# Turning the mixed values of three groups by DMA transposes in two 16-bit planes instead of on TensorE

## The chip, the cores and the metric

The kernel runs on one core of one Trainium2 chip. The metric is device time in microseconds, as the median of several executions; beside it stands one execution taken by the hardware profiler, whose rows are quoted here. The engines are TensorE (PE, with its weight loads PEld), VectorE (DVE), ScalarE (ACT), GpSimd (POOL) and SyncE (SP). SP computes nothing; it issues nearly all DMAs, in order. Each engine runs its own list of instructions in order and waits on semaphores of the others.

## What is computed

One layer of a decoder on 256 tokens of width 2048, float32. Cut to the part around the change:

```python
h = rmsnorm(x, norm_mix_w)
q, k, v, z, b_raw, a_raw, p_in, g_a, g_b = split(h @ w_in)
# q, k, v: causal convolution of width 4, silu; q, k normalised
o   = gated_delta_rule(q, k, v, g_log, beta)            # 16 heads of 128
y_a = rmsnorm(o, gdn_norm_w) * silu(z)
y_b = (trailing means of p_in, 4 groups of 512) @ pool_w[group] * pool_scale
mixed = sigmoid(g_a) * y_a + sigmoid(g_b) * y_b         # 256 x 2048
x = x + mixed @ w_out
# then: rmsnorm, gated MLP of 5632 with a causal convolution, w_down, final rmsnorm
```

## The kernel before

**Products of two parts.** TensorE multiplies in a rounded format (`F32R`). To keep float32 accuracy every operand is held as a high part (the value rounded) and a low part (the rest), and a product is the sum of high x high, low x high and high x low. Activations are split once. Weights are split as they stream: SP loads a weight tile of 256 rows by 512 columns (512 KB) into `raw` (line 122, four buffers), ACT makes `whi` by a cast (line 141, three buffers), DVE makes `wlo` as the difference (line 149, three buffers). This happens in `begin`, called by `weights`, two tiles ahead of use (`AHEAD`, line 29). A raw buffer comes free when its `wlo` is made; a `whi` or `wlo` buffer when PE has used the tile.

**GEMMs.** `gemm_a` (lines 168 to 186) goes through the weight tiles of a product with 512 output columns: for each tile twelve matmuls, lines 179 to 181, of which only line 181 reads `wlo`. The first matmul of a tile therefore waits for ACT's cast, the third for DVE's difference. A GEMM over the width of 2048 has eight tiles.

**Order of the groups.** The mixer runs in four groups `g` of four heads (512 channels). A group runs GEMMs for k, q, v, pooling input, gate b, the pooling weights, z and gate a. Work that hangs on a GEMM's result is not placed right behind it but put on a list, `later`, whose entries are called inside the next GEMM, when its second weight tile begins. A second list, `side_work`, holds the delta rule of the group (`gdn`) as a generator, of which a step is taken with every half tile. A scheduler then orders each engine's instructions by its own estimates of their times; the call order above is what it starts from, and tiles of a pool are given out in that order.

**The place of the change.** When a group's delta rule is done, `gated` (line 901) forms the group's mixed values in `sz` with two DVE operations (lines 903 and 904): 128 partitions, two token tiles `t`, 512 channels. The output projection needs them with channels on the partitions. `mixed` (line 913), put on `later` for groups 0 to 2 (line 920) and called at once for group 3, does that: `turned` (line 216) makes eight TensorE transposes of 128x128 into two PSUM tiles from the pool `psg` (line 224; four buffers, used by the delta rule and the convolutions too), ACT casts each PSUM tile to the high part `mhi` (line 916) and DVE subtracts for the low part `mlo` (line 917). Both are read first by the two unfinished output GEMMs `early`, after all four groups' GEMMs. `turned` is also used by `conv_silu` for the results `ev` of the k and q GEMMs.

**Queues.** SP's list holds, in order, the raw loads; per group two loads of convolution weights (`taps`, line 573) into the buffers named `sz` and `yb`; a store of v to memory and three shifted loads back (lines 855 and 587); and small copies of the delta rule through memory (`cdd`, `lb`, `tbd`, `TT`: lines 703, 706, 725, 728). Buffers of the pool `mp` have one copy for most names: `ga0` holds decayed products of the group's delta rule, `yb` the pooled branch, both free once `sz` is formed and taken again by the next group's taps or delta rule.

Of the kernel before, what the change touches and what calls it, by code (L numbers as in the profile page):

```python
# [6 lines left out]

F32 = mybir.dt.float32
F32R = mybir.dt.float32r
I32 = mybir.dt.int32  # L10
AF = mybir.ActivationFunctionType
ALU = mybir.AluOpType

P = 128
S = 256
# [18 lines left out]
def kernel(  # L34
# [20 lines left out]
    nc = tc.nc  # L55
# [11 lines left out]
    def nm(s):  # L67
        cnt[0] += 1
        return f"{s}_{cnt[0]}"

    def pg(shape=(P, 512)):
        return psg.tile(list(shape), F32, tag="g", name=nm("psg"))
# [85 lines left out]
    def drain():  # L158
        for _ in side_work[0]:
            pass  # L160
# [5 lines left out]
    later = []  # L166

    def gemm_a(lh, ll, nk, steps=None, ps=None):

        ps = pm() if ps is None else ps  # L170
        for c in range(nk // 2) if steps is None else steps:
            if c == 1:
                while later:
                    later.pop(0)()
            hi, lo = weights()
            for kk in range(2):
                k = 2 * c + kk
                for t in range(2):
                    mm(ps[:, t, :], lh(k, t), hi[:, kk, :], start=(k == 0), stop=False)  # L179
                    mm(ps[:, t, :], ll(k, t), hi[:, kk, :], start=False, stop=False)  # L180
                    mm(ps[:, t, :], lh(k, t), lo[:, kk, :], start=False, stop=(k == nk - 1))  # L181
                side()
        return ps
# [32 lines left out]
    def turned(src):  # L216

        out = []
        for f2 in range(2):
            pt = pg([P, 2, S])  # L220
            for ff in range(2):
                f = 2 * f2 + ff
                for t in range(2):
                    nc.tensor.transpose(pt[:, ff, t * P : (t + 1) * P], src[:, t, f * P : (f + 1) * P], ident)
            out.append(pt)
        return out


# [20 lines left out]
    mp = mix.__enter__()  # L249
# [193 lines left out]
    for g, w in enumerate(WINDOWS):  # L443
# [13 lines left out]
                            op=ALU.add)  # L457
# [100 lines left out]
    def evict(ps, by=None):  # L558

        by = rs1 if by is None else by  # L560
        e = mp.tile([P, 2, 512], F32, tag="ev", bufs=1, name=nm("ev"))
        for t in range(2):
            nc.scalar.activation(e[:, t, :], ps[:, t, :], AF.Copy, scale=by[:, t : t + 1])
        return e
# [25 lines left out]
    def v_conv(g, vt):  # L590

        vt = vt.rearrange("p t h d -> p t (h d)")
        for j, m in zip((2, 1, 0), moved_of[g]):
            nc.vector.tensor_tensor(m, m, taps_of[g][j], op=ALU.mult)
            nc.vector.tensor_tensor(vt, vt, m, op=ALU.add)
            yield
        th = mp.tile([P, 2, 512], F32, tag="th", name=nm("th"))
        nc.scalar.activation(th, vt, AF.Tanh)
        yield
        nc.vector.scalar_tensor_tensor(vt, th, 1.0, vt, op0=ALU.add, op1=ALU.mult)  # L600
        yield

    def conv_silu(e, kind, g, dst):

        pts = turned(e)
        y = mp.tile([P, 4, S], F32, tag="cy", bufs=2, name=nm("cy"))
        for f in range(4):
            r = kind * 16 + 4 * g + f
            gs = pts[f // 2][:, f % 2, :]

            def w(j):
                return cqw[:, j * 48 + r : j * 48 + r + 1]

            nc.scalar.activation(y[:, f, :], gs, AF.Copy, scale=w(3))
            for j in (2, 1, 0):
                s = 3 - j
                nc.vector.scalar_tensor_tensor(y[:, f, s:], gs[:, : S - s], w(j), y[:, f, s:],
                                               op0=ALU.mult, op1=ALU.add)
        th = mp.tile([P, 4, S], F32, tag="th", name=nm("th"))
        nc.scalar.activation(th, y, AF.Tanh)  # L620
        k_conv.append(nc.vector.scalar_tensor_tensor(dst, th, 1.0, y, op0=ALU.add, op1=ALU.mult).ins)
# [214 lines left out]
    for g in range(4):  # L836
        kq = mp.tile([P, 4, 2, S], F32, tag="kq", bufs=1, name=nm("kq"))
        for kind, dst in ((1, kq[:, :, 0, :]), (0, kq[:, :, 1, :])):
            ps = ps_k0 if kind == 1 and g == 0 else gemm_a(xh, xl, KD)
            e = evict(ps)  # L840
            later.append(lambda e=e, kind=kind, g=g, dst=dst: conv_silu(e, kind, g, dst))

        vt = mp.tile([P, 2, 4, P], F32, tag="vt", name=nm("vt"))
        vt2 = vt.rearrange("p t h d -> p t (h d)")
        res = []
        later.append(lambda g=g, kq=kq, vt=vt, res=res: side_work.__setitem__(0, gdn(g, kq, vt, v_conv(g, vt), res)))
        v_taps(g)
        if g == 0:
            def after_k(k_conv=k_conv[0]):
                with tc.issue_after(last_pow[0]), tc.issue_after(k_conv):  # L850
                    fixed_parts()

            later.append(after_k)
        e = evict(gemm_a(xh, xl, KD), rsh)
        nc.sync.dma_start(vrow[g, SH : SH + S, :].rearrange("(t p) d -> p t d", p=P), e)
        later.append(lambda e=e, g=g, vt2=vt2: v_moved(e, g, vt2))


        win = WINDOWS[g]
        psb = scales(g)  # L860
        ps = gemm_a(xh, xl, KD)
        e = evict(ps)
        phi = mtile(g, [P, 4, S], F32R, nm("phi"))
        plo = mtile(4 + g, [P, 4, S], F32R, nm("plo"))

        def pooled(e=e, g=g, phi=phi, plo=plo):
            for f2 in range(2):
                pt = pg([P, 2, S])
                for ff in range(2):
                    fs = slice((2 * f2 + ff) * P, (2 * f2 + ff + 1) * P)  # L870
                    mm(pt[:, ff, P:S], e[:, 1, fs], bands[:, g, P + PAD : NB], start=True, stop=False,
                       skip_group_check=True)
                    mm(pt[:, ff, 0 : P + PAD], e[:, 0, fs], bands[:, g, 0 : P + PAD], start=False, stop=True,
                       skip_group_check=True)
                fs = slice(2 * f2, 2 * f2 + 2)
                nc.scalar.copy(phi[:, fs, :], pt)
                nc.vector.tensor_tensor(plo[:, fs, :], pt, phi[:, fs, :].bitcast(F32), op=ALU.subtract)

        later.append(pooled)

        def gate(ps, tag):
            th = mp.tile([P, 2, 512], F32, tag=tag, name=nm("gate"))
            for t in range(2):
                nc.scalar.activation(th[:, t, :], ps[:, t, :], AF.Tanh, scale=rsh[:, t : t + 1])
            return th

        tb = gate(gemm_a(xh, xl, KD), "th")
        ps = gemm_a(lambda k, t: phi[:, k, t * P : (t + 1) * P], lambda k, t: plo[:, k, t * P : (t + 1) * P], 4)
        yb = mp.tile([P, 2, 512], F32, tag="yb", name=nm("yb"))
        nc.vector.tensor_tensor(yb, ps, psb.unsqueeze(1).to_broadcast([P, 2, 512]), op=ALU.mult)  # L890
        nc.vector.scalar_tensor_tensor(yb, tb, 1.0, yb, op0=ALU.add, op1=ALU.mult)

        ps = gemm_a(xh, xl, KD)
        sz = mp.tile([P, 2, 512], F32, tag="sz", name=nm("sz"))
        nc.vector.scalar_tensor_tensor(sz, gate(ps, "th"), 1.0, ps, op0=ALU.add, op1=ALU.mult)
        ta = gate(gemm_a(xh, xl, KD), "th")
        nc.vector.scalar_tensor_tensor(sz, ta, 1.0, sz, op0=ALU.add, op1=ALU.mult)
        sz4 = sz.rearrange("p t (h d) -> p (t h) d", h=4)
        nc.vector.tensor_tensor(sz4, sz4, gwb.unsqueeze(1).to_broadcast([P, 8, P]), op=ALU.mult)

        def gated(sz=sz, res=res, yb=yb):
            drain()
            nc.vector.tensor_tensor(sz, res[0].rearrange("p t h d -> p t (h d)"), sz, op=ALU.mult)
            nc.vector.tensor_tensor(sz, sz, yb, op=ALU.add)

        if g < 3:
            gated()
        mh = mtile(g, [P, 4, S], F32R, f"mhi{g}")
        ml = mtile(4 + g, [P, 4, S], F32R, f"mlo{g}")
        mhi.append(mh)  # L910
        mlo.append(ml)

        def mixed(sz=sz, mh=mh, ml=ml):
            for f2, pt in enumerate(turned(sz)):
                fs = slice(2 * f2, 2 * f2 + 2)
                nc.scalar.copy(mh[:, fs, :], pt)
                nc.vector.tensor_tensor(ml[:, fs, :], pt, mh[:, fs, :].bitcast(F32), op=ALU.subtract)

        if g < 3:
            later.append(mixed)  # L920

    def at(tiles):
        return lambda k, t: tiles[k // 4][:, k % 4, t * P : (t + 1) * P]
# [46 lines left out]
    for c in range(DFF // 512):  # L970
# [4 lines left out]
        for f in range(4):  # L975
# [3 lines left out]
            for j in (1, 0):  # L979
                s = 2 - j  # L980
# [114 lines left out]
```

## Time and profile before

| | |
|---|---|
| median of 3 executions | 1572.16 us (1571.49 to 1575.03) |
| the profiled execution, own time | 1572.57 us |
| its span, first to last instruction | 1570.8 us |
| granted TensorE clock, mean | 0.998 |
| share of the 16 DMA engines' time by SP's queue | 61.0% |
| data moved | 304.23 MB, 194 GB/s |

The page gives busy times per engine, and the span in 40 slices of 39 us with the busy share of each in tenths. A timeline row is: start in us from the span's start, length, engine, line, operation, output and inputs, shapes, count. A row of a group by line is: line, engine, operation, tile names, shapes, count, then busy us and mean ns of one, then the idle time ahead of it and what ended that. Lengths of PE rows are those of pipelined matmuls, which overlap; the distance between two starts is what one costs. The three turns of mixed values on PE begin at 243.8, 420.8 and 599.1 us; that of group 3 at 769 to 771 us.

### The profile page before, as it was taken

The page shows a single profiled execution, that of the slowest core. Times are in us where ns is not written, and L with a number is a line of the kernel's source. Part 1 is how long each engine was busy: PE and PEld are TensorE (multiplying, and loading weights), DVE is VectorE, ACT ScalarE, POOL GpSimd, SP SyncE. Part 2 cuts the span into 40 slices and gives each one's busy share as a digit, 9 for nine tenths or more (in the row PEclk, how much of TensorE's full clock was granted, in tenths as well). Part 3 has the DMA queues.
Part 4 walks back from the last instruction along what each step waited for, and adds up shares of the span by engine and source line. Part 5 has one row for each costly group of instructions (what it writes and reads, how often), then busy time and mean ns, then how long its engine had stood idle before and what let it go on. Part 6 is the DMA issues. An engine that isn't in the chain of part 4 may idle for free.

```text
span 1570.8 us, 21247 instructions
## 1 busy us (share of the span) xinstructions
PE 1558.3 (99%) x8022; PEld 1308.1 (83%) x8022; DVE 1077.4 (69%) x1647; ACT 744.7 (47%) x956; POOL 47.4 (3%) x69
## 2 busy tenths in 40 slices
PE   9999999999999999999999999999999999999997
PEld 8878888888887888888888888888888888888886
DVE  6897849796797758796656667766666667444444
ACT  6554446444554445544454544444444445334443
POOL 2110000000010001000000000000000000000000
PEclk9999999999999999999999999999999999999999
DMA  8676747666666756775555556555555566556662
GB/s 272 199 219 194 207 148 218 201 207 176 183 211 185 210 159 192 214 205 177 198 191 183 188 189 190 188 189 187 187 189 188 188 188 216 198 190 208 203 223 90
DMA packets 168229, 304.23 MB, mean 194 GB/s; under 512 B 19234, under 2 KB 22834, under 8 KB 167998
## 3 DMA queue, kind: packets, MB, share of 16 engines
q1 hardware_dynamic: 165104, 297.84, 61.0%
q10 hardware_dynamic: 3022, 5.03, 0.9%
q8 instruction: 63, 1.03, 0.3%
q14 instruction: 40, 0.33, 0.1%
HBM read 297.56 MB, written 5.27 MB: 193 GB/s over the span
## 4 chain that ended last, share of the span: by engine, by line
PE 50%; issue 1%; ACT 0%; DVE 0%; POOLq 0%; POOL 0%
PE psm L203 10%; PE psg L203 10%; PE psg L204 5%; PE psm L204 5%; PE psg L1008 2%; PE psg L1010 2%; PE psg L1009 2%; PE psm L1010 2%; PE psm L1008 2%; PE psm L1009 2%; PE psm L180 1%; PE psm L181 1%; PE psm L179 1%; PE psg L954 0%; ACT xt L1037 0%
## 5 line engine op out<-in xcount | busy, mean ns | idle before, releaser
L149 DVE TENSOR_TENSOR wlo<-raw,whi 128x1024 fp32r<-128x1024 f32 x522 | 636.9, 1222 | 379.2 <-ACT whi L141 373.6
L141 ACT CAST whi<-raw 128x1024 fp32r<-128x1024 f32 x524 | 550.8, 1053 | 715.1 <-PE psm L180 305.7
L181 PE MATMUL psm<-wlo,xhl 128*128 128x512 f32 x864 | 340.3, 394 | 1.1 <-DVE wlo L149 1.1
L179 PE MATMUL psm<-whi,xhl 128*128 128x512 f32 x864 | 339.6, 393 | 0.0
L180 PE MATMUL psm<-whi,xhl 128*128 128x512 f32 x864 | 338.2, 391 | 0.0
L203 PE MATMUL psm<-fhl,whi 128*128 128x512 f32 x704 | 246.2, 396 | 0.0
L203 PE MATMUL psg<-fhl,whi 128*128 128x512 f32 x704 | 238.0, 394 | 0.0
L204 PE MATMUL psm<-fhl,wlo 128*128 128x256 f32 x704 | 194.4, 279 | 0.0
L181 PEld LDWEIGHTS psm<-wlo,xhl 128*128 128x128 f32 x864 | 162.3, 188 | 34.8 <-DVE wlo L149 1.9
L180 PEld LDWEIGHTS psm<-whi,xhl 128*128 128x128 f32 x864 | 162.3, 188 | 33.2
L179 PEld LDWEIGHTS psm<-whi,xhl 128*128 128x128 f32 x864 | 162.3, 188 | 33.0 <-issue 0.5
L204 PE MATMUL psg<-fhl,wlo 128*128 128x256 f32 x704 | 178.7, 279 | 0.0
L203 PEld LDWEIGHTS psm<-fhl,whi 128*128 128x128 f32 x704 | 131.4, 188 | 30.5
L203 PEld LDWEIGHTS psg<-fhl,whi 128*128 128x128 f32 x704 | 129.2, 188 | 24.2
L204 PEld LDWEIGHTS psg<-fhl,wlo 128*128 128x128 f32 x704 | 132.5, 188 | 6.9
L204 PEld LDWEIGHTS psm<-fhl,wlo 128*128 128x128 f32 x704 | 132.5, 188 | 1.1
L1008 PE MATMUL psg<-whi,hhi 128*128 128x512 f32 x168 | 65.5, 390 | 0.0
L1008 PE MATMUL psm<-whi,hhi 128*128 128x512 f32 x168 | 65.4, 389 | 0.0
L1009 PE MATMUL psm<-whi,hlo 128*128 128x512 f32 x168 | 65.4, 389 | 0.0
L1010 PE MATMUL psm<-wlo,hhi 128*128 128x512 f32 x168 | 65.4, 389 | 0.0
L1009 PE MATMUL psg<-whi,hlo 128*128 128x512 f32 x168 | 65.4, 389 | 0.0
L1010 PE MATMUL psg<-wlo,hhi 128*128 128x512 f32 x168 | 59.1, 389 | 0.0
(263 smaller groups left out, 1527.2 us busy)
## 6 DMA issues: line engine op xcount, KB each, us to landing
raw<-in_w_in_dram SPq DMA_DIRECT2D x224, 512.0 KB, 4.2
raw<-in_w_up_dram SPq DMA_DIRECT2D x176, 512.0 KB, 4.6
raw<-in_w_down_dram SPq DMA_DIRECT2D x88, 512.0 KB, 4.3
raw<-in_w_out_dram SPq DMA_DIRECT2D x32, 512.0 KB, 3.7
mv<-vrow SPq DMA_DIRECT2D x12, 512.0 KB, 5.8
taps<-in_conv_qkv_w_dram SPq DMA_DIRECT2D x16, 256.0 KB, 5.6
raw<-in_pool_w_dram SPq DMA_DIRECT2D x8, 512.0 KB, 5.3
vrow<-ev SPq DMA_DIRECT2D x4, 512.0 KB, 3.1
```

The lines of the kernel that those rows point to most:

```text
L141: nc.scalar.copy(hi, raw)
L149: nc.vector.tensor_tensor(lo, raw, hi.bitcast(F32), op=ALU.subtract)
L179: mm(ps[:, t, :], lh(k, t), hi[:, kk, :], start=(k == 0), stop=False)
L180: mm(ps[:, t, :], ll(k, t), hi[:, kk, :], start=False, stop=False)
L181: mm(ps[:, t, :], lh(k, t), lo[:, kk, :], start=False, stop=(k == nk - 1))
L203: mm(ps[f], hi[:, kk, fs], rhl(k), start=(k == 0), stop=False, skip_group_check=True)
L204: mm(ps[f][:, 1, :], lo[:, kk, fs], rhl(k)[:, 0, :], start=False, stop=(k == nk - 1), skip_group_check=True)
L1008: mm(acc[c][t], lh(k, t), hi[:, kk, :], start=(k == 0), stop=False)
L1009: mm(acc[c][t], ll(k, t), hi[:, kk, :], start=False, stop=False)
L1010: mm(acc[c][t], lh(k, t), lo[:, kk, :], start=False, stop=(k == KF - 1))
```

## The change

For groups 0 to 2 the turn no longer runs on TensorE. `sz` is viewed as 16-bit halves. For each half `z` ACT copies the plane of that half (every second 16-bit element, 1024 per partition) to a buffer; SP issues two DMA transposes of it, one per token tile, each of 128 partitions by 4 x 128 elements of 16 bits (128 KB), into another part of the same buffer; and DVE copies the two results into every second 16-bit element of a float32 tile `turned`, 512 elements each. When all four joins are done, ACT casts the tile whole to `mhi` and DVE subtracts whole for `mlo`. The planes take the buffer named `ga0`, the turned tile the one named `yb`. Group 3 goes on using TensorE.

```diff
+    def turned_by_dma(src):
+
+        src = src.bitcast(U16).rearrange("p t (f z) -> p t f z", z=2)
+        pl = mp.tile([P, 2, 2, 2 * 512], U16, tag="ga0", name=nm("planes"))
+        out = mp.tile([P, 4, S], F32, tag="yb", name=nm("turned"))
+        to = out.bitcast(U16).rearrange("p f (t s z) -> p t f s z", t=2, z=2)
+        for z in range(2):
+            a = pl[:, 0, z].rearrange("p (t f) -> p t f", t=2)
+            b = pl[:, 1, z].rearrange("p (t f s) -> p t f s", t=2, f=4)
+            nc.scalar.copy(a, src[:, :, :, z])
+            for t in range(2):
+                nc.sync.dma_start_transpose(b[:, t], a[:, t])
+            for t in range(2):
+                nc.vector.tensor_copy(to[:, t, :, :, z], b[:, t])
+        return out
...
+        def mixed_by_dma(sz=sz, mh=mh, ml=ml):
+            m = turned_by_dma(sz)
+            nc.scalar.copy(mh, m)
+            nc.vector.tensor_tensor(ml, m, mh.bitcast(F32), op=ALU.subtract)
+
...
         if g < 3:
-            later.append(mixed)
+            later.append(mixed_by_dma)
```

Lines behind the new helper move by 16. In the compiled order of the changed kernel, each group's four transposes stand in a row on SP's list, behind a raw load and ahead of two loads of taps and the next raw load; the order of DVE and ACT around them is told where the prediction uses it.

2 lines of the change are left out of this document (1 added, 1 removed).

## Prediction

> **What bounds the kernel now.** I read the page first: span, busy times, the slices.
>
> ```profile
> span 1570.8 us, 21247 instructions
> PE 1558.3 (99%) x8022; PEld 1308.1 (83%) x8022; DVE 1077.4 (69%) x1647; ACT 744.7 (47%) x956; POOL 47.4 (3%) x69
> ...
> DVE  6897849796797758796656667766666667444444
> ```
>
> PE is busy for 99% of the span, DVE fills 90% or more of single slices of the first half. A busy share of PE says little by itself, so the waits of PE come next:
>
> ```profile
> PE psm L181 <- DVE wlo L149: 2.1, 2, 1.1
> PE psm L240 <- POOL ones L230: 1.1, 1, 1.1
> PE psm L180 <- DVE mlo L917: 0.6, 1, 0.6
> PE psm L179 <- ACT mhi L916: 0.5, 1, 0.5
> ```
>
> PE waits 4.3 us in the whole run. So the time is the sum of what PE issues, and an edit counts by what it takes off PE's list, or by the wait for DVE, ACT or a load that it makes. The windows around the three places where mixed values are turned:
>
> ```profile
> 228.00:268.00 40.00, 40.00 (x201) 33.71 (x200) 34.06 (x60) 22.75 (x34) 3.16 (x4) 1.00 0.60 179
> 405.00:445.00 40.00, 40.00 (x201) 33.72 (x200) 34.08 (x60) 22.78 (x33) 3.15 (x4) 1.00 0.64 188
> 583.00:623.00 40.00, 40.00 (x201) 33.81 (x200) 32.97 (x57) 22.36 (x33) 4.95 (x4) 1.00 0.67 187
> ```
>
> The columns are the length, then busy us of PE, weight loads, DVE, ACT, POOL, the granted clock, the DMA share, GB/s. PE has no gap, DVE about 6 us of slack in 40, ACT 17.
>
> **The change part by part.** *Removed from PE:* eight transposes in each of groups 0 to 2; the eight of group 3 stay. The timeline of PE at group 0 (start, length, instruction):
>
> ```profile
> 242.89 0.39 PE L180 MATMUL psm<-whi,xhl 128*128 128x512 f32 x1
> 243.12 0.39 PE L181 MATMUL psm<-wlo,xhl 128*128 128x512 f32 x1
> ...
> 243.80 1.03 PE L224 MATMUL psg<-ident,sz 128*128 128x128 f32 x8
> 244.67 1.04 PE L224 MATMUL psg<-ident,ev 128*128 128x128 f32 x8
> 245.47 0.48 PE L181 MATMUL psm<-wlo,xhl 128*128 128x512 f32 x1
> ```
>
> From the start of the eight of `sz` to the start of the next eight are 0.87 us; three groups give **-2.6 us**. The same rows give the pace of a weight tile: a matmul every 0.23 us, twelve per tile, 2.72 us.
>
> *Exchanged on ACT and DVE.* The groups by form (count | busy us, mean ns), and the timeline of DVE just after the turn, with two rows of ACT:
>
> ```profile
> L149 DVE TENSOR_TENSOR wlo<-raw,whi 128x1024 fp32r<-128x1024 f32 x522 | 636.9, 1222 | 379.2 <-ACT whi L141 373.6 <-PE psg L224 4.5
> L141 ACT CAST whi<-raw 128x1024 fp32r<-128x1024 f32 x524 | 550.8, 1053 | 715.1 <-PE psm L180 305.7 <-PE psm L203 127.8 <-PE psg L203 92.2
> L917 DVE TENSOR_TENSOR mlo<-psg,mhi 128x512 fp32r<-128x512 f32 x8 | 5.1, 682 | 0.0
> L916 ACT CAST mhi<-psg 128x512 fp32r<-128x512 f32 x8 | 4.3, 588 | 0.2
> L224 PE MATMUL psg<-ident,sz 128*128 128x128 f32 x32 | 4.1, 272 | 0.0
> L715 DVE COPY tb<-idb 128x256 f32<-128x256 f32 x4 | 1.2, 292 | 3.0 <-DMA tbd<-tb 2.5 <-POOL idb L435 0.5
> ```
>
> ```profile
> 244.40 1.23 DVE L149 TENSOR_TENSOR wlo<-raw,whi 128x1024 fp32r<-128x1024 f32 x1 [1.49 <-PE psg L224]
> 245.54 1.28 DVE L917 TENSOR_TENSOR mlo<-psg,mhi 128x512 fp32r<-128x512 f32 x2
> 246.74 2.42 DVE L617 SCALAR_TENSOR_TENSOR cy<-psg,cqw,cy 128x255 f32<-128x255 f32 x6
> 249.08 1.21 DVE L149 TENSOR_TENSOR wlo<-raw,whi 128x1024 fp32r<-128x1024 f32 x1
> ...
> 254.23 1.05 ACT L141 CAST whi<-raw 128x1024 fp32r<-128x1024 f32 x1 [1.39 <-issue]
> 255.18 1.06 ACT L620 ACTIVATE th<-cy 128x1024 f32<-128x1024 f32 x1
> ```
>
> (The mean of 272 ns of a transpose of `sz`, taken 24 times, would give 6.5 us for the step before; they overlap, so the starts are what counts.) ACT loses two casts of 0.59 and gains three passes over 1024 elements (two splits, one cast) at 1.05: +2.0 us a group, in 17 us of slack. DVE loses two subtractions of 0.68 and gains four joins of 512 elements and a subtraction of 1.22. No row shows a 16-bit copy with a step: it lies between the copy of 256 elements (0.29) and an operation on 512 (0.68); I take 0.68, the row of its size, so DVE gets +2.6 us a group, in 6 us of slack. The Trainium skill ("VectorE: DVE Perf Modes", "What auto-detection actually checks") admits the packed 16-bit mode only where every tensor has step 1, which the joins' output has not; that is on the side of the upper end, and no run here shows it.
>
> *The wait that is added.* DVE works in order, and in the compiled order of the changed kernel, group 0, its first join (waiting for transpose 1) stands ahead of a `wlo`; ACT's cast `mhi` (waiting for join 4) stands ahead of a `whi`. PE waits for these two, with two finished weight tiles in hand. I lay the new order out with the spacings above (cast 0.95, `wlo`, `kq` or `mlo` 1.14, join 0.60, `cy` 0.39, the small `r` about 0.28), from the start of split 1. These rows give the last one, and the matmuls of `r`, two of which PE runs in front of some tiles:
>
> ```profile
> 259.51 0.79 DVE L643 TENSOR_SCALAR r<-tri,ghi 128x128 fp32r<-128x128 f32 x2
> 260.22 0.47 DVE L617 SCALAR_TENSOR_TENSOR cy<-psg,cqw,cy 128x255 f32<-128x255 f32 x1
> 260.61 0.47 DVE L643 TENSOR_SCALAR r<-tri,glo 128x128 fp32r<-128x128 f32 x2
> 261.00 0.47 DVE L617 SCALAR_TENSOR_TENSOR cy<-psg,cqw,cy 128x255 f32<-128x255 f32 x1
> ...
> L651 PE MATMUL psg<-r,lowr 128*128 128x256 f32 x16 | 3.7, 280 | 0.0
> ```
>
> ACT: splits at 0 and 0.95, `th` at 1.9, cast B at 2.9. Transpose 1 can go out at 1.05. DVE: `kq` (waits for `th`) 3.0 to 4.1, two `r`, join 1 at 4.7, `wlo` B done at 6.5, join 2, two `cy`, joins 3 and 4 until 9.0, `wlo` C done at 10.2, two `cy`, three `r`, `mlo` until 12.9, five `r`, two `cy`, `wlo` D done at 16.3. PE, with 2.72 a tile, 0.80 for the eight of `ev` and 0.12 to 0.23 for each matmul of `r`, needs B at 9.0 to 9.5, C at 12.2 to 13.1, D at 15.0 to 15.8. So B and C are 2 us or more early, D is 0.5 to 1.3 late, without any wait for DMA: a pile-up of DVE work. In groups 1 and 2 the joins alternate with `wlo`, and the same laying out leaves 0 to 0.5. I take **+0.7 us** for the three together.
>
> *Price of the chain of transposes.* Four of 128 KB each, one behind another on SP, which no trace shows. DMA rows of before (KB each, us to landing), and two issues of SP:
>
> ```profile
> raw<-in_w_in_dram SPq DMA_DIRECT2D x224, 512.0 KB, 4.2
> vrow<-ev SPq DMA_DIRECT2D x4, 512.0 KB, 3.1
> lb<-cdd SPq DMA_DIRECT2D x16, 128.0 KB, 5.6
> cdd<-ga SPq DMA_DIRECT2D x32, 16.0 KB, 1.5
> ...
> 244.87 0.82 SPq L573 DMA_DIRECT2D taps<-in_conv_qkv_w_dram  x2
> ```
>
> SP takes 0.41 us an issue. Lowest: three more issues and the landing of `cdd`, 1.2 + 1.5 = 2.7 us from the first issue to the last landing. Highest: four landings of `lb` one after another, 22.4. Nearest row: `lb` itself, 128 KB, four issued in a row, so 1.2 + 5.6 = **6.8 us**. What the order can hide: for D to be no later than it is, `mhi` must end by 15.4 - 1.2 - 0.8 - 1.4 - 1.1 = 10.9 (the mean deadline less `wlo`, two `cy`, five `r`, `mlo`), so join 4 by 9.8 and the last landing by 9.2, that is 8.1 us after the first issue at 1.05. With 6.8 the chain is hidden by DVE's own list; beyond **about 8 us** each us is a us of PE, in three groups.
>
> *SP's queue.* Behind the four stand two loads of taps (needed two GEMMs later) and the next raw load. It is wanted by a cast some 12 us after split 1 and takes 4.2, so SP may be held until about 8: four issues of up to 1.7 us are free. The 512 KB more a group are 7% of the 7.2 MB that 179 GB/s move in a window, at a DMA share of 0.60.
>
> *Buffers.* The planes lie where `ga0` was, the turned values where `yb` was; the next users come two GEMMs later, and two PSUM tiles a group come free, which lets the next convolution begin earlier. I cost both at nothing; the mixed halves themselves are first read after group 3's GEMMs.
>
> **Sum.** Own time of the profiled execution 1572.6 (span 1570.8 and 1.8 around it): 1572.6 - 2.6 + 0.7 = 1570.7. It lies 0.4 above the median 1572.2, so **1570.3** against the median.
>
> **The rivals.**
> 1. *The gain is eaten (1571.6 to 1574).* DVE's extra 2.6 us come in the fullest stretch; if D is late by its upper 1.3 in each group, +3.9 - 2.6. For it: DVE has no idle between 244.4 and 249.1. Against: 6 us of slack in each window.
> 2. *Late chain, slower (1574 to 1585, and far beyond).* The mechanism is the one above: joins hold `wlo`, `mhi` holds `whi`. It decides at a chain of 8 us, and is slower on balance from about 8.7. At 12 us: 3 x 4 - 2.6 + 0.7, 1582. At the upper end, 22.4: 3 x 14.4 - 1.9, about 1613. For it: `lb` is only 1.3 us below the point. Against: half of `lb`'s landing is its queue of four, counted already.
>    The Trainium skill speaks against the change here: "VectorE: DVE Perf Modes", "The three transpose paths", gives 1309 ns for a 128x128 transpose by the DMA crossbar and 390 ns by TensorE, and advises TensorE where PSUM will do. If that is per block, the sixteen blocks of a group make a chain of 20.9 us and a time near 1609; if it is the cost of one DMA, 5.2 and a landing, near the point. PE's own rows (0.11 us each) are below its figure for TensorE. The page "DMA: Bandwidth & Descriptors", "Latency and other measured facts", gives 261 GB/s, an estimate of 0.5 us a transpose, hidden.
> 3. *More than the list (below 1569).* With earlier convolutions one of the two 1.1 us waits for `wlo` goes too and D is in time: -2.6 - 1.1, 1568.5.
> 4. *It doesn't do what it says:* if the transposes stayed on PE; the compiled order has only group 3's eight left, so no chance of its own.
>
> **How the numbers follow.** Forecast (1568.8 to 1571.6): 0.42. Eaten: 0.16. Late chain to 1585: 0.26. Far beyond, by landings one after another: 0.08. Below 1569 by rival 3: 0.08. 0.2% is 3.1 us, about what a measurement of this kernel can tell from no change: faster is below 1569.0, slower above 1575.3. Faster: rival 3 and 0.07 of the forecast, 0.15. Slower: 0.23 of the late chain and the 0.08, 0.31. Same: 0.54. The range 1568.2 to 1582 leaves out the far end, a part of the late chain and a little of rival 3; most chance lies on both sides of no change, and the likeliest case alone has 1568.8 to 1571.6.
>
> **What would show it.** Right: eight transposes left under `sz`; no wait of PE for `wlo` above 1.3 us near 250, 427 and 605; joins of at most 0.7 us; the last of the four landing within 8 us of the first issue. Wrong: a DMA transpose that holds SP over 1.7 us; DVE idle before a join while PE waits for the `wlo` behind it; ACT idle before `mhi` with PE waiting for a `whi`; a raw load landing late after the four.

## The result: slower by 0.2%, and the profile after

The changed kernel takes 1575.71 us (median of 17 executions, 1573.07 to 1578.92), the kernel before 1571.88 us beside it (17 executions, 1570.88 to 1575.03): a ratio of 1.0023, 95% interval 1.0016 to 1.0030, or +3.6 us. The forecast was 1570.3; the time is inside the range, on the other side of no change.

The profiled execution of the changed kernel has an own time of 1574.45 us, 1.3 below its median. Its page, the lines that answer to those of before:

```profile
span 1572.4 us, 21226 instructions
...
PE 1557.8 (99%) x7998; PEld 1305.5 (83%) x7998; DVE 1080.5 (69%) x1656; ACT 748.8 (48%) x959; POOL 44.7 (3%) x69
```

PE has 24 matmul rows fewer and is busy for 0.5 us less, and yet the span is 1.6 us longer. The waits of PE (what, how often, the longest):

```profile
PE psm L181 <- DVE wlo L149: 2.7, 6, 0.9
PE psg L670 <- ACT dec L671: 1.1, 1, 1.1
PE psm L256 <- POOL ones L246: 1.1, 1, 1.1
PE psm L180 <- DVE mlo L938: 0.6, 1, 0.6
PE psm L179 <- ACT mhi L937: 0.5, 1, 0.5
PE psm L179 <- ACT whi L141: 0.3, 1, 0.3
```

Two are new: a wait for `whi` and one for `dec`, both of ACT; those for `wlo` went from two to six. The windows around the three turns, with the columns of before:

```profile
228.00:268.00 40.00, 39.65 (x197) 33.31 (x196) 35.27 (x67) 24.60 (x38) 3.78 (x5) 1.00 0.69 186
405.00:445.00 40.00, 38.63 (x190) 32.05 (x189) 34.31 (x65) 23.17 (x36) 4.79 (x5) 1.00 0.65 186
583.00:623.00 40.00, 39.47 (x194) 32.74 (x193) 31.56 (x56) 24.23 (x36) 3.75 (x5) 1.00 0.63 186
```

PE now has gaps of 0.35, 1.37 and 0.53 us there, 2.25 together, where it had none. The passes of the turn, splits and joins, are as priced or cheaper. The tile `planes` and the users of `sz` (count, then the shortest, median and longest in ns):

```profile
L239 SPq DMA_TRANSPOSE planes<-planes x12: 1220/1264/2154, 245.9 to 603.1; - x12
L241 DVE COPY turned<-planes x12: 450/460/666, 250.7 to 607.2; 128x512 uint16<-128x512 uint16 x12
L237 ACT COPY planes<-sz x6: 1039/1045/1048, 244.8 to 599.1; 128x1024 uint16<-128x1024 uint16 x6
...
DMA to landing us min/median/max: 2.4/3.2/4.1
```

```profile
L224 PE MATMUL psg<-ident,sz x8: 270/272/273, 771.5 to 772.2; 128*128 128x128 f32 x8
```

What is late is a raw load. SP's timeline at the first turn, then ACT's casts that wait for the raw tile behind the transposes, in all three groups (in brackets the idle time ahead and what ended it), then PE:

```profile
242.01 3.42 SPq L122 DMA_DIRECT2D raw<-in_w_in_dram  x2
245.90 5.67 SPq L239 DMA_TRANSPOSE planes<-planes  x4
251.62 1.30 SPq L589 DMA_DIRECT2D taps<-in_conv_qkv_w_dram  x2
253.03 2.60 SPq L122 DMA_DIRECT2D raw<-in_w_in_dram  x3
...
429.68 3.07 SPq L122 DMA_DIRECT2D raw<-in_w_in_dram  x4
...
606.63 3.12 SPq L122 DMA_DIRECT2D raw<-in_w_in_dram  x4
```

```profile
254.17 1.05 ACT L931 CAST mhi<-turned 128x1024 fp32r<-128x1024 f32 x1 [2.36 <-DVE turned L241]
...
259.18 1.05 ACT L141 CAST whi<-raw 128x1024 fp32r<-128x1024 f32 x1 [2.22 <-DMA raw<-in_w_in_dram]
...
436.46 1.05 ACT L141 CAST whi<-raw 128x1024 fp32r<-128x1024 f32 x1 [2.94 <-DMA raw<-in_w_in_dram]
...
613.72 1.05 ACT L141 CAST whi<-raw 128x1024 fp32r<-128x1024 f32 x1 [4.29 <-DMA raw<-in_w_in_dram]
```

```profile
437.56 0.50 PE L179 MATMUL psm<-whi,xhl 128*128 128x512 f32 x1 [0.29 <-ACT whi L141]
...
439.67 0.51 PE L670 MATMUL psg<-r,onesr 128*128 128x256 f32 x2 [1.08 <-ACT dec L671]
...
616.08 0.50 PE L181 MATMUL psm<-wlo,xhl 128*128 128x512 f32 x1 [0.53 <-DVE wlo L149]
```

The transposes hold SP for 5.67 us, two loads of taps for 1.30 more, and the next raw load goes out at 253.03, 7.1 us after the first transpose. The cast that waits for it starts 6.2 us later (259.18; 6.8 and 7.1 in the other groups). ACT stands for 2.2, 2.9 and 4.3 us, and behind the late cast stand in ACT's list `dec`, for which PE waits 1.08 us at 439.67, and in DVE's the `wlo` of 616.08. ACT's waits for tiles from `w_in` in the whole run, before and after:

```profile
ACT whi L141 <- DMA raw<-in_w_in_dram: 8.4, 3, 4.4
ACT whi L141 <- DMA raw<-in_w_in_dram: 20.0, 7, 4.4
```

Not all of this lies at the turns. The 8.4 us of before lie between 60 and 104 us, ahead of the first turn. Of the 20.0 after, 8.7 lie there too, 9.5 at the three turns and 1.8 at 282 us.

There is a second place, 23 to 30 us behind the first transpose of each turn: the round trip of v through memory (the store `vrow`, the shifted loads `mv`, the first product with them). In group 2, before:

```profile
629.51 0.37 SPq L855 DMA_DIRECT2D vrow<-ev  x1
629.97 0.42 SPq L122 DMA_DIRECT2D raw<-in_w_in_dram  x1
632.62 1.40 SPq L587 DMA_DIRECT2D mv<-vrow  x3
...
638.12 1.23 DVE L594 TENSOR_TENSOR mv<-mv,taps 128x1024 f32<-128x1024 f32 x1 [1.69 <-DMA mv<-vrow]
```

and after:

```profile
629.44 0.37 SPq L871 DMA_DIRECT2D vrow<-ev  x1
629.91 0.41 SPq L122 DMA_DIRECT2D raw<-in_w_in_dram  x1
635.68 1.39 SPq L603 DMA_DIRECT2D mv<-vrow  x3
...
639.74 1.23 DVE L610 TENSOR_TENSOR mv<-mv,taps 128x1024 f32<-128x1024 f32 x1 [2.98 <-DMA mv<-vrow]
640.88 1.22 DVE L149 TENSOR_TENSOR wlo<-raw,whi 128x1024 fp32r<-128x1024 f32 x1
```

From the store's issue to the first product are 8.61 us before and 10.30 after; `mv` is issued only when `vrow` has landed. DVE stands meanwhile (1.69 and 2.98 us), with differences `wlo` behind the product in its list. Added up over the three groups that have a turn ahead of them, the round trips take 23.6 us before and 28.6 after: 7.3, 7.7 and 8.6 against 8.2, 10.1 and 10.3. This sum is used below.

### The profile page after: what moved, and what is told of

It is laid out like the page before. It is cut to its first block, busy times and chain, and to the rows that moved or that the text cites. A ratio compares the mean times of both kernels' runs of the same rounds, so it can differ in the third digit from the quotient of the medians.

```text
span 1572.4 us, 21226 instructions
## 1 busy us (share of the span) xinstructions
PE 1557.8 (99%) x7998; PEld 1305.5 (83%) x7998; DVE 1080.5 (69%) x1656; ACT 748.8 (48%) x959; POOL 44.7 (3%) x69
## 4 chain that ended last, share of the span: by engine, by line
PE 50%; issue 1%; ACT 0%; DVE 0%; POOLq 0%; POOL 0%
PE psm L203 10%; PE psg L203 10%; PE psg L204 5%; PE psm L204 5%; PE psg L1029 2%; PE psg L1030 2%; PE psg L1031 2%; PE psm L1029 2%; PE psm L1030 2%; PE psm L1031 2%; PE psm L180 1%; PE psm L181 1%; PE psm L179 1%; PE psg L975 0%; ACT xt L1058 0%
```

## The experiments

**The theories.** T1: SP's queue is the loss; it is held by the transposes, the raw load behind them is late, and what hangs on it. T2: the extra passes and the joins' waits for the landings pile up in the in-order lists of ACT and DVE. T3: the scheduler orders the rest anew, and that order is worse whatever SP does. Later a fourth was needed, T4: the bytes of the transposes slow the other loads.

"Stand" is the time from the first of the group's new DMAs on SP to the next raw load, mean of the three groups; "raw" is the total wait of ACT's cast in line 141 for tiles from `w_in`, the part far from the turns included; "v" is the sum of the three round trips. All but the ratio are from each run's profiled execution. (In two groups of e14 a raw load goes out between the two copies, so the stand is short there.)

| run | edit of the changed kernel | stand, us | ratio to before, 95% | raw | v |
|---|---|---|---|---|---|
| changed | none | 7.3 | 1.0023 (1.0016 to 1.0030) | 20.0 | 28.6 |
| e1 | no turn at all | 0 | 0.9995 (0.9986 to 1.0004) | 13.9 | 23.7 |
| e2 | passes, no DMA | 0 | 0.9995 (0.9987 to 1.0004) | 6.8 | 23.4 |
| e3 | DMAs, nobody waits | 7.1 | 1.0045 (1.0031 to 1.0059) | 23.4 | 31.3 |
| e4 | each DMA twice, nobody waits | 14.0 | 1.0185 (1.0171 to 1.0199) | 21.8 | 24.9 |
| e5 | five raw buffers | 7.2 | 1.0005 (0.9996 to 1.0014) | 5.3 | 28.9 |
| e6 | before, five raw buffers | - | 0.9992 (0.9983 to 1.0000) | 0 | 24.1 |
| e7 | transposes issued by ACT | - | 1.0156 (1.0142 to 1.0170) | 6.8 | 24.7 |
| e8 | second plane later | 7.1 | 1.0030 (1.0020 to 1.0041) | 6.8 | 29.9 |
| e9 | plain copies, with waits | 4.8 | 1.0032 (1.0020 to 1.0044) | 14.0 | 24.8 |
| e10 | taps issued by POOL | 5.5 | 1.0056 (1.0044 to 1.0068) | 17.8 | 29.9 |
| e11 | before, taps issued by POOL | - | 1.0014 (1.0005 to 1.0022) | 5.1 | 23.2 |
| e12 | e10 with five raw buffers | 6.0 | 1.0058 (1.0045 to 1.0072) | 0.3 | 28.5 |
| e13 | hold without bytes | 10.2 | 1.0131 (1.0117 to 1.0145) | 23.9 | 24.5 |
| e14 | bytes with little hold | 1.6 | 1.0000 (0.9991 to 1.0009) | 8.6 | 23.9 |
| e15 | none, a second time | 7.3 | 1.0028 (1.0018 to 1.0039) | 15.9 | 29.8 |
| e16 | two transposes for four | 4.6 | 1.0020 (1.0011 to 1.0028) | 11.7 | 29.2 |
| e17 | e16 with five raw buffers | 4.8 | 1.0013 (1.0004 to 1.0022) | 0 | 28.3 |
| e18 | plain copies, nobody waits | 4.6 | 1.0014 (1.0005 to 1.0023) | 15.4 | 25.2 |

**e1 and e2: the passes without DMAs.** e1 hands `sz` unturned to the last cast and subtraction; e2 keeps splits and joins and leaves the DMAs out, so that its values stay unturned too.

```diff
 e1  -  m = turned_by_dma(sz)
     +  m = sz.rearrange("p t (a s) -> p (t a) s", a=2)
 e2  -  nc.sync.dma_start_transpose(b[:, t], a[:, t])
     -  nc.vector.tensor_copy(to[:, t, :, :, z], b[:, t])
     +  nc.vector.tensor_copy(to[:, t, :, :, z], a[:, t].rearrange("p (f s) -> p f s", f=4))
```

> Leaves out the turn of groups 0 to 2: high and low parts are made from sz as it lies, so the output is not the reference's. No transposes on TensorE, no splits, no DMAs, no joins; one cast and one subtraction a group stay. Theory 1 (the raw weight loads behind the transposes and taps on SP's list land late, and ACT's cast and then PE wait): nothing of that is left, 2 to 3 us below the kernel before. Theory 2 (splits and joins pile up in DVE's and ACT's lists, joins wait for DMA): the same, 2 to 3 us below. Theory 3 (the scheduler's new order of the rest costs, whatever replaces the turn): within 1.5 us of the kernel before.

> Leaves out the DMA transposes alone: splits on ACT and joins on DVE stay, the joins read the planes untransposed, so the output is not the reference's. Theory 1: 1.5 to 2.5 us below the kernel before, PE without a wait for wlo above 0.6 us near the three turns. Theory 2 by the passes: 2 to 4 us above, as the changed kernel is. Theory 3: within 1.5 us.

1571.25 and 1570.99 us, before 1572.01. The passes cost nothing that can be measured (e2 against e1); that half of T2 falls. Without any DMA the kernel is 0.8 to 1.0 us ahead of before, of the 2.6 that PE no longer issues, with an interval that takes in zero. So T1, which had 2 to 3 us and 1.5 to 2.5 us here, misses in both, and T3's 1.5 us holds. In e1's profile PE waits 3.6 us for `wlo`, before 2.1: a part of what the transposes left free comes back as stalls elsewhere.

**e3 and e4: the DMAs, with nobody waiting.** The joins read the unturned plane, so no instruction waits for a transpose; e4 issues each one twice.

```diff
 e3  -  nc.vector.tensor_copy(to[:, t, :, :, z], b[:, t])
     +  nc.vector.tensor_copy(to[:, t, :, :, z], a[:, t].rearrange("p (f s) -> p f s", f=4))
 e4  as e3, and
     -  for t in range(2):
     +  for t in (0, 1, 0, 1):
```

> The transposes are issued and land, but the joins read the untransposed planes, so nobody waits for them; the output is not the reference's. Theory 1: SP is still held and the raw load behind is late, 1.5 to 4 us above the kernel before, ACT waits for raw loads over 2 us at each turn. Theory 2 by the wait for landings: 1.5 to 2.5 us below. Theory 3: within 1.5 us.

> As the run before, with every transpose issued twice: eight in a row a group, nobody waits; output not the reference's. Theory 1: SP is held 4 x 1.26 us longer a group, the raw load later by as much, nearly all of it on PE: 10 to 18 us above the kernel before. Theory 2 and theory 3: no more than 2 us from the run before.

1579.23 and 1601.06 us. Taking the waits away gains nothing, so the waits of T2 are not the loss here. But e3 is 7.2 us above the kernel before (medians), more than any of the three theories had (T1: 1.5 to 4). In its profile PE stands longest far from a turn: 3.2 us at 465, for a `wlo` behind `mv`. Doubling the DMAs adds 21.8 us. That makes 29 us above before, where T1 had 10 to 18. SP and PE of e4 at the first turn:

```profile
245.17 12.24 SPq L239 DMA_TRANSPOSE planes<-planes  x8
257.46 1.99 SPq L589 DMA_DIRECT2D taps<-in_conv_qkv_w_dram  x4
259.50 15.40 SPq L122 DMA_DIRECT2D raw<-in_w_in_dram  x7
```

```profile
261.65 0.39 PE L181 MATMUL psm<-wlo,xhl 128*128 128x512 f32 x1
269.89 0.79 PE L179 MATMUL psm<-whi,xhl 128*128 128x512 f32 x1 [7.85 <-ACT whi L141]
```

The raw load goes out 14.3 us after the first transpose, and PE, out of weights, stands for 8.0 us (7.2 and 7.5 at the other turns).

**e5 and e6: a fifth raw buffer**, in the changed kernel and, as a control, in the kernel before.

```diff
-  raw = wpool.tile(..., tag="raw", bufs=4)
+  raw = wpool.tile(..., tag="raw", bufs=5)
-  dg = cpool.tile([P, P], F32, tag="diag", bufs=2, ...)
+  dg = cpool.tile([P, P], F32, tag="diag", bufs=1, ...)
-  idh = mp.tile([P, P], F32, name="idh")
+  idh = mp.tile([P, P], F32, tag="jk", name="idh")
```

> The changed kernel with five buffers of raw weights in place of four (room for it is made by one buffer of diag in place of two, and by idh taking a buffer that is in use at another time), to be read against the same edit on the kernel before (e6). With one more buffer a raw load can be issued one weight tile earlier, so a list of SP that stands for 5.7 us of transposes and 1.3 to 2.1 us of taps is made up before a cast asks. The theory that SP's queue is the loss: ACT's waits for raw fall back to 15 us or less and the time is 0.5 to 2 us below that of e6. The theory that the scheduler's new order of the rest is the loss: 2 to 4 us above e6, as the change is above the kernel before.

> The kernel before with the same five buffers of raw weights: the control of e5. Its PE waits for weights are small already, so 0 to 2 us below the kernel before by both theories; by how far it differs from the kernel before is to be taken off e5.

1573.04 against 1570.84: by the medians the change costs 2.2 us where it cost 3.8. Loads that can go out a tile earlier shorten ACT's waits for raw at the turns from 9.5 to 5.3 us (those at 60 to 104 us go with the fifth buffer, in e6 too), and PE's stalls at 437 and 616 are gone, as T1 says. By the time, though, this is the lower end of T3's case: v stays at 28.9, and the largest stall left, 2.2 us at 286, is a `wlo` behind `mv`. So there is more than the late raw load.

**e7: the transposes on ACT's queue.**

```diff
-  nc.sync.dma_start_transpose(b[:, t], a[:, t])
+  nc.scalar.dma_start_transpose(b[:, t], a[:, t])
```

> The changed kernel with its DMA transposes issued by ACT in place of SP. The traffic is the same, SP is not held, and ACT stands for some 5 us a group instead. The theory that SP's queue is the loss: the raw loads are issued in time, but the weight casts of the same stretch stand behind the transposes on ACT; ACT has about half of its time free and the raw tiles are there already, so 1570 to 1573 us, and ACT's waits for raw are at 15 us or less. The rival that the traffic of the transposes makes the raw loads land late: ACT's waits for raw stay at 20 us or more, and the time is at 1575 or more. If the hold of 5 us on ACT costs as much as that on SP, the time is 1575 to 1580 with no waits for raw.

1596.83 us. The waits for raw at the turns are gone (the 6.8 us left lie at 60 to 102 us), but ACT itself stands for 6.3 us in a row at the first turn, and makes no `whi` meanwhile. ACT's idle half is not idle at that place. The time is above all three cases. My lowest case, that ACT's slack would hide the hold, was wrong.

**e8: the second plane one GEMM later** (split, transposes, joins and cast of `z` = 1 put on `later` behind the next GEMM).

> The changed kernel with the second plane (split, two transposes, two joins) and the cast behind it handed out one matrix product later, so that SP is held by two transposes at a time. The theory that SP's queue is the loss: a hold of 2.5 us is within what the next raw load has to spare, the waits for raw go back to 15 to 18 us, and the time is 1570.5 to 1573. The theory that the new order of the rest is the loss: it stays at 1574 to 1577. The rival that the traffic is the loss: about the same traffic in two halves, 1572.5 to 1574.5.

1576.64 us, but it does not test what it was meant to: the scheduler put the four transposes in a row all the same (5.58 us, stand 7.1). By the names in the traces SP, DVE and PE work through the same lists as in the changed kernel, so this is in effect that kernel once more, and it costs as much: the raw tiles are late again (the 6.8 us are those of two turns, 2.8 and 4.0) and v is 29.9.

**e9 and e18: plain copies**, with the joins waiting and without. The values stay unturned.

```diff
 e9  -  nc.sync.dma_start_transpose(b[:, t], a[:, t])
     +  nc.sync.dma_start(b[:, t], a[:, t].rearrange("p (f s) -> p f s", f=4))
 e18 as e9, and the joins read a[:, t] as in e3
```

> The changed kernel with each DMA transpose replaced by a plain DMA copy of the same 128 x 512 values of 16 bits between the same two tiles (the values stay unturned; all else is computed). Bytes, passes and waits stay, and SP should be held by about 0.4 us a copy, as by the other loads on its list, in place of 1.26. The theory that the hold of SP is the loss: SP is through with the four after about 2 us, ACT's waits for raw go back to 15 us or less, and the time is 1571 to 1572.5, like that without DMAs (e2). The rival that it is the traffic or the wait of the joins for the landings: 1574.5 to 1577, like the changed kernel.

> e9 with joins that read the unturned plane and so wait for nothing (e9 and e14 differ in two things, the four issues in place of two and the waits of the joins; here only the four issues are left). If the waits for the landings are what e9 lost by: 1571 to 1573.5, like e14. If four issues of 0.6 us with the taps behind them are enough: 1575 to 1579, like e9.

1577.96 and 1573.99 us. e9 misses what T1 expected of it (1571 to 1572.5). The four copies hold SP for 2.4 to 2.5 us, not for 2, and to the raw load behind the taps pass another 2.2 to 2.6, so that the stand is still 4.8 us of 7.3. e18 lies between its two cases. Beside it, the waits of the joins would be worth about 3 us here (1.0032 against 1.0014, with intervals that overlap), while e3 against the changed kernel shows them worth nothing. Differences of this size between builds are not explained by one cause.

**e10, e11 and e12: the taps issued by POOL**, in the changed kernel, in the kernel before, and with five raw buffers.

```diff
-  nc.sync.dma_start(tp[:, i, :], conv_qkv_w...)
+  nc.gpsimd.dma_start(tp[:, i, :], conv_qkv_w...)
```

> The changed kernel with the loads of taps issued by POOL in place of SP, to be read against e11, where only that is done to the kernel before. SP's list keeps the transposes, but no taps stand between them and the next raw load, which is issued 1.3 to 2.1 us earlier. The theory that SP's list is the loss: about a third of it goes, so 1 to 2.5 us above e11 where it was 3.6. The rival that it is the new order of the rest: 3 us or more above e11.

> The kernel before with the loads of taps issued by POOL: the control of e10. SP issues four DMAs of 0.4 us fewer a group, and its raw loads had little to wait for: 1570 to 1572.5 by every theory, unless DMAs on POOL cost something of their own.

> The changed kernel with both: five buffers of raw weights and the taps issued by POOL. If SP's list is all that the change loses by, the two together give what the change without its DMAs gave, and the extra buffer's own gain with it: 1569.5 to 1571. If a part of the loss is the new order of the rest (late wlo far from the turn), it stays at 1572 or more, as with the five buffers alone.

1579.71, 1573.84 and 1581.43 us. T1 misses in both builds with the change, T3's cases hold. e11 itself is above its 1570 to 1572.5, so loads issued by POOL cost something of their own. On SP the stand is shorter (5.5), yet the change costs 5.9 us over its control. Beside the loads from POOL the transposes land after 5.8 us in the median, not 3.2, and v is 29.9. e12 has 0.3 us of waits for raw left, and gains nothing by it.

**e13 and e14: hold and bytes apart.** e13 replaces each transpose by three DMAs of one row of 1 KB; e14 replaces the four by one plain copy for each plane. In both the joins read the unturned plane, as in e3.

```diff
 e13 -  nc.sync.dma_start_transpose(b[:, t], a[:, t])
     +  for n in range(3):
     +      nc.sync.dma_start(b[n : n + 1, t], a[n : n + 1, t].rearrange("p (f s) -> p f s", f=4))
 e14 -  for t in range(2):
     -      nc.sync.dma_start_transpose(b[:, t], a[:, t])
     +  nc.sync.dma_start(pl[:, 1, z], pl[:, 0, z])
```

> As e3 (nobody waits, joins read the unturned plane), but each transpose replaced by three DMAs of one row of 1 KB: SP should be held about as long as by the transposes (12 issues of 0.4 us a group), with next to no bytes moved. The theory that the hold of SP makes the loss, by late raw loads and then by the round trip of V's rows through DRAM that runs into the loads being made up: 1576 to 1581, near the 1579.2 of e3, with the three round trips from the store of V's rows to the first product with them at 27 us or more together, where the kernels without DMAs of planes had 23.2 to 24.1. The rival that it is the bytes: 1570.5 to 1572.5, like e2, with round trips of 24 us.

> As e3, but the four transposes of a group replaced by two plain copies of a whole plane each: the same bytes, SP held by two issues in place of four long ones, about 1.2 us in place of 5.2. The theory that the hold of SP is the loss: 1570.5 to 1573, with round trips of V's rows of 24.5 us or less. The rival that it is the bytes: 1575 to 1580.

1592.83 and 1573.00 us beside 1572.63 before. The same number of bytes in plain copies with little hold cost nothing; next to no bytes with a long hold cost 20 us. T4 falls as far as it is about bytes; that a long hold costs time is shown. e13 holds SP longer than I had aimed at (0.7 us an issue, not 0.4), and costs more than the 1576 to 1581 expected. SP and PE of e13:

```profile
246.12 8.48 SPq L240 DMA_DIRECT2D planes<-planes  x12
254.65 2.01 SPq L590 DMA_DIRECT2D taps<-in_conv_qkv_w_dram  x4
256.70 5.18 SPq L122 DMA_DIRECT2D raw<-in_w_in_dram  x4
```

```profile
262.60 0.39 PE L181 MATMUL psm<-wlo,xhl 128*128 128x512 f32 x1
267.28 0.80 PE L179 MATMUL psm<-whi,xhl 128*128 128x512 f32 x1 [4.29 <-ACT whi L141]
```

With a stand of 10.6 us PE's distance from start to start is 4.68 us where 0.23 is usual, so 4.5 are lost; with 14.3 (e4) it is 8.24, so 8.0. 3.7 us more of stand give 3.5 us more of stall. At the six turns of the two runs the stand is 4.9 to 6.5 us longer than the stall, but this cannot be carried over to the changed kernel as it is. In e13 and e4 four loads of taps stand ahead of the raw load, not two, and from the raw load's issue to its cast are 9.1 to 9.7 us, where the changed kernel has 6.2 to 7.1. Counted from the first new DMA to the start of that cast, PE had 14.6 to 15.9 us free in e13 and e4; the changed kernel has 13.3, 14.0 and 14.5. It stands just short of that point, and what PE loses there is mostly not the wait for the late cast (0.29 us at 437.56) but for what stands behind it (`dec`, `wlo`). A part of my expectation failed: I had v at 27 or more, and it is 24.5. Where PE itself stands for long (e4, e7, e13), v is short again.

**e15: the changed kernel once more.**

> The changed kernel once more, unaltered, beside the other two on one chip, for a second profile of the same program: the waits for raw at the three turns and the long round trips of V's rows should come again by the theory of SP's hold (20 us or more of ACT's waits for raw, 27 us or more of round trips), while the stalls behind the solve's loads, which the kernel before has too, may fall elsewhere. Time 1574 to 1577.5.

1576.81 us. The same stalls come again: ACT waits 2.05, 2.80 and 4.26 us for the three raw tiles (in all 15.9, less than the 20 expected), and v is 29.8.

**e16 and e17: one transpose for a whole plane**, two in a group in place of four, with the kernel's full result; e17 has five raw buffers too.

```diff
-  for t in range(2):
-      nc.sync.dma_start_transpose(b[:, t], a[:, t])
+  nc.sync.dma_start_transpose(pl[:, 1, z].rearrange("p (n s) -> p n s", n=8), pl[:, 0, z])
```

> The changed kernel with one DMA transpose of a whole plane (128 x 1024 values of 16 bits) in place of two of half a plane: the same bytes and the same result with two issues a group. If the hold of SP goes by the issue, it is 2.5 us a group in place of 5.2, the next raw load is issued some 2.6 us earlier, under the hold at which the others began to cost, and the time is 1570 to 1573. If it goes by the bytes, SP is held as long as before and the time is 1574 to 1577.5.

> e16 with five raw buffers, to be read against e6 (five raw buffers, no change: 0.9992 of the kernel before) and e5 (1.0005). With a shorter hold and one more buffer the theory of SP's hold gives the change's gain without its loss: 1569 to 1571.5. If the hold is as long as before: 1571.5 to 1574, like e5.

The tile `planes` of e16:

```profile
L238 SPq DMA_TRANSPOSE planes<-planes x6: 1257/1305/1344, 245.4 to 608.0; - x6
...
DMA to landing us min/median/max: 4.8/4.9/5.1
```

The hold goes by the issue: 1.31 us for 128x1024 values, 1.26 for 128x512. The two hold SP for 2.7 us, and no cast at the turns makes PE wait any more. Still the times are 1574.94 and 1574.21, beyond what T1 gave for a short hold (1573 and 1571.5). What is left is v (29.2 and 28.3). The profiled executions of e16 and e17 are the slowest of their eleven (1578.06 and 1577.74), so a usual one can have lost less at the place that follows. DVE and PE of e16:

```profile
460.58 1.22 DVE L609 TENSOR_TENSOR mv<-mv,taps 128x1024 f32<-128x1024 f32 x1 [6.27 <-DMA mv<-vrow]
...
465.55 1.22 DVE L149 TENSOR_TENSOR wlo<-raw,whi 128x1024 fp32r<-128x1024 f32 x1
```

```profile
462.60 0.39 PE L180 MATMUL psm<-whi,xhl 128*128 128x512 f32 x1
466.82 0.79 PE L181 MATMUL psm<-wlo,xhl 128*128 128x512 f32 x1 [3.83 <-DVE wlo L149]
467.41 0.63 PE L179 MATMUL psm<-whi,xhl 128*128 128x512 f32 x1
```

PE stands 4.0 us longer here than usual, for a `wlo` that is queued behind `mv`.

**What is shown, and what stays open.** Shown: the passes cost nothing that can be measured (e2), nor do the bytes as plain copies (e14); without the waits for the landings nothing is gained (e3), though e9 beside e18 leaves some 3 us in doubt for copies; and a long stand of SP costs PE nearly as much as it is made longer (e13, e4). In the changed kernel the rows lead from the stand to PE: its stalls behind the late raw loads (437.56, 439.67 and 616.08, each less the usual distance) are 2.4 us together, and 2.3 in e15, about what the change takes off PE's list.

Open is the rest. Where PE no longer waits at the turns (e5, e12, e16, e17), stalls behind `mv` stand in the place of those at the turn, and some 2 us or more of loss remain beside the controls. v is 23.2 to 24.1 in the kernels without DMAs of planes (before, e1, e2, e6, e11), 23.9 to 25.2 with plain copies (e9, e14, e18), and 28.3 to 31.3 in all with transposes on SP in which PE did not stand for long, even where the stand of SP was only 4.6 us. That `vrow` or `mv` land later is seen; why, only in part. In group 1 of the changed kernel two raw loads, not one, stand in SP's list between the store and the shifted loads (so too in e5, e8, e10, e12 and e15), and from the first shifted load's issue to the first product are 6.2 us, not 3.6. In group 2 SP's list there is that of before, but the last raw load goes out 0.90 us ahead of the store, not 3.16, and the shifted loads can follow the store only after 6.24 us, not 3.11. So it is in all the runs: with a raw load issued at most 1.3 us ahead of the store, the shifted loads follow after 4.3 to 7.5 us (11 round trips); with none for 2.5 us, after 2.8 to 4.4 (28). e13, without transposes, has one of the first kind (0.42 and 5.32), so they are not needed for it. Why the raw loads stand closer to the store in most builds with transposes stays open. The builds with transposes and those with copies also differ in the order of some 200 instructions (the changed kernel and e9), since the scheduler plans by its own estimate of a DMA. The runs do not separate that order (T3) from something that transposes do.

No version of the change with the full result beats the kernel before. The fastest is the kernel before with a fifth raw buffer (e6), 0.9992, whose interval ends at 1.0000.

## Why the prediction was wrong, point by point

It failed at two places that it put at nothing: SP's queue behind the transposes, and the lists far from the turn.

- **PE's 2.6 us: right as a step, not as a gain.** The 24 transposes are gone (eight rows under `sz` are left), but e1 and e2 brought 0.8 to 1.0 us of it to the end, not 2.6.
- **ACT and DVE: right, and cheaper.** Splits 1.045 us (1.05 taken), joins 0.46 (0.68 taken, the nearest row of its size; between the two bounds), and they cost nothing that can be measured (e2 against e1). The rule of the Trainium skill ("VectorE: DVE Perf Modes", "What auto-detection actually checks") that a stepped output stays out of the packed mode is neither borne out nor refuted by this: there is no row of the same copy with step 1.
- **Weight tile D late, +0.7: about right.** PE has one stall of 0.5 us in group 0 for that reason (260.83, `wlo` behind `r` and `cy`, no wait for a DMA ahead of it); e5 and e15 have it too, 0.56 and 0.34.
- **The chain, 6.8 us and hidden up to 8: right in effect, its size by luck.** The three further issues took 3.9 to 4.8 us, not 1.2, and a landing 3.2 us in the median (2.4 to 4.1), not 5.6; the two errors nearly cancel. The last join of group 0 starts by 253.7, at most 7.8 us after the first issue, and waits for nothing; that of group 2 starts at 607.2, 8.0 us after it, just at the bound. `mhi` waits 2.36 us for the joins at 254.17, and PE does not notice. In e3, without the waits, nothing is gained.
- **SP's queue: the step that failed.** "SP may be held until about 8: four issues of up to 1.7 us are free." The issues were 1.26 us, under the bound, and were not free. The sum was that the cast wants the raw tile 12 us after split 1 and the landing takes 4.2. Two of its terms were too small. The two loads of taps, named as standing behind the four, were given no time: they take 1.0 to 2.1 us, and the raw load goes out 8.2 to 8.5 us after split 1. The larger miss is the landing, taken at the median row: from the raw load's issue to the cast are 6.2, 6.8 and 7.1 us, with two loads of taps issued just ahead of it. In e13, with four taps ahead and next to no bytes of planes, they are 9.2 to 9.7, so the planes need not be the reason. The cast starts 14.3, 15.1 and 15.6 us after split 1, where 12 were reckoned. PE's stalls behind it are 2.4 us.
- **Buffers and places far from the turn at nothing: wrong.** The prediction ended at the turn. The round trips of v 23 to 30 us later are 5 us longer together, and DVE's list has `wlo` behind them; that part is seen in the builds with transposes, and it remains when PE no longer waits at the turns (e5, e17). This second step failed too, and its cause is the one left open above.
- **The rivals.** "Late chain, slower" had the right side and the wrong mechanism: DVE and ACT do wait for joins and landings, but PE not behind them. The figure of "The three transpose paths" in "VectorE: DVE Perf Modes" of the Trainium skill, 1309 ns for a 128x128 transpose by the crossbar, does not hold here as a price per block: a DMA of four or eight blocks costs 1.26 or 1.31 us of issue and lands after 3.2 or 4.9 us (medians). That it is close to the time of one issue may be chance. In the list of what would show it wrong, the last entry was the one: a raw load landing late after the four.

## What to carry over

A queue that issues DMAs is an in-order engine: for each load behind an inserted DMA, add up what every issue ahead of it takes, those already there too, and the landing under the load of that stretch, not its median. A wait can be hidden and the issue still be paid. When such a gain of a few us is planned, look also at the next round trip through memory, because lists that were ordered around its old time do not move with it.

## What the runs showed of the hardware

- **Issue time, not bytes.** A DMA transpose of 16-bit values within SBUF holds SP for 1.26 us at 128x512 and 1.31 at 128x1024 (medians); plain copies of the first size 0.59 us, one-row DMAs 0.59 (0.71 from one to the next in a row of twelve), a load of taps 0.41 before the change and up to 1.62 behind the transposes. The Trainium skill, "DMA: Bandwidth & Descriptors", "Issuing engines are not separate DMA queues", calls the sequencer's time for an issue usually small relative to the DMA itself; here 1.26 us of issue stand beside 3.2 from issue to landing, and the issues rather than the bytes made the cost (e13 against e14).
- **A stall of 2 us or more can cost a second time.** After PE's 4.0 us in e16, the granted clock is half for 5.6 us. The window of that run:

```profile
466.80:472.40 5.60, 5.58 (x13) 4.42 (x14) 5.60 (x8) 1.99 (x2) 1.84 (x1) 0.50 0.67 183
```

  13 matmuls where 0.23 us each would take 3.0: 2.6 us more. The length alone does not decide it. Stalls of 2.16, 2.20 and 2.28 us (e10, e5, e3; distance from start to start less 0.23) did not do it; 2.04 (e17), 2.27 (e14) and 2.45 (e10, e12) did, and so did the long ones of e13 and e4. The Trainium skill ("TensorE: Matmul & The Clock Gate", "Part 1: The HAM clock gate") gives an idle window of about 3.4 us, free-running. The runs agree with a gate that halves the clock (in e17 for 3.4 us, from 288.7 to 292.1), and show it after shorter gaps. Whether this adds to the scatter of the changed kernel (1573.1 to 1578.9, before 1570.9 to 1575.0) is open: its two profiles show no stall of over 1.3 us near or behind the turns, and no half clock there.
